# Keeping the low halves of the up weights in DRAM for the second half of the sequence

## The chip, the cores and the metric

The kernel runs on one core of a Trainium2 chip. The time is the device time of one execution in microseconds (us); smaller is better. The engines are TensorE (PE in the profile; PEld is its weight load), VectorE (DVE), ScalarE (ACT), GpSimd (POOL), and SyncE (SP), which here issues every DMA.

## The reference

One layer of a bidirectional hybrid encoder, in float32, for 2048 rows of width 1024:

```
mod = silu(c) @ w_ada + b_ada                       # shift1, scale1, gate1, shift2, scale2, gate2
u = adaln_modulate(x, shift1, scale1);  proj = u @ w_in
attn = rms_norm(gqa_attention(q, k, v))             # 8 query heads, 2 kv heads, axial rope
h = rms_norm(silu(layer_norm(depthwise_conv(a * sigmoid(g), width 31))) @ w_conv_pw2)
x = layer_norm(ALPHA * x + gate1 * (concat(attn, h) @ w_o))
u = adaln_modulate(x, shift2, scale2)
val, gt = split(depthwise_conv(u @ w_up, width 3))  # w_up: 1024 x 5632
x = layer_norm(ALPHA * x + gate2 * ((gelu(gt) * val) @ w_down))
```

The part that the change touches is `u @ w_up`, with the start of it inside the output projection `@ w_o` and the preparation of `w_down` beside it.

## The kernel before

Each float32 matrix product is made of three products of split numbers: an operand x is written as a high part (`wh` for weights, a rounded copy made by ACT, L124) and a low part (`wl`, x minus the high part, made by DVE, L127), and PE adds high*high, high*low and low*high.

The up projection and the down projection are block products of Strassen's kind: a 2 x 2 block product with seven products instead of eight (the numbers 0 to 6 are q in the code). A *set* is one block of this. In the up projection there are 44 sets: for each half of the sequence (1024 rows) 22 blocks of weights, each holding 128 gate columns and 128 value columns. The second half goes through the weight blocks in reverse order, so that sets 21 and 22 use the same block, whose prepared weights are kept in SBUF. A set has 7 products of 12 matmuls of 128 x 512.

- `wprep(n)` prepares the weights (the left operands) of set n. Two raw tiles `wr` of 512 KB come from `w_up`; DVE forms the sums and differences (`s`, and `wr` in place; L1068, L1071, L1072, L1082), and `put` splits each of the seven results into `wh` and `wl`. `run_set(n)` does the seven products and after each one calls the next step of `wprep(n + 1)`. The tiles `wh` and `wl` have seven buffers each, so the buffer of product q of the next set comes free when product q of this set is done.
- `evac` brings a finished product out of PSUM: DVE additions (L1126, L1129, L1133) and ACT copies (L1118, L1124).
- `post(n)` does the width-3 convolution, the GELU and the gate of the set before on ACT and DVE (L1139 to L1171) and stores the result `y` to `g_d`.
- `feed(q)` splits the right operand of product q (tiles `o`, from `stg`, four pieces of 128 x 512) for a whole half of the sequence. For the first half, operands 0 to 2 are made during the output projection (`ahead`), and operands 3 to 6 in set 0.
- `combine(1)` forms the right operands of the second half on POOL during sets 1 to 3 (`cb`, L917, L919). `down_ops` then scales the 22 row blocks of `w_down` on POOL, forms their sums and differences and stores them to `w_d` (L1187 to L1198); it goes one step after each product of even number, from set 3 on.

The output projection goes through 16 row tiles t. For each there are 48 matmuls (`out_mm`), then `norm1(t)` on DVE and ACT, and `second_in(t)`: eight transposes on PE, eight small ACT copies (`ut`) and a store to `u_d`. The last two `second_in` lie inside set 0.

The program is written with a framework that orders each engine's instructions by a simulated time; so each engine, and SP with its DMAs, has one fixed order, and an instruction that waits holds up those behind it on its engine. An operation placed earlier in the code can be placed much earlier on its engine, if its inputs allow.

Of the kernel before, what the change touches and what calls it, by code (L numbers as in the profile page):

```python
# [18 lines left out]
P = 128  # L19
# [7 lines left out]
NJ = DFF // P  # L27
# [6 lines left out]
def layer_kernel(ctx, tc, x, cT, w_ada, b_ada, b_adaT, w_in, qg2, kg2, rope, conv_t, cmask, mmask,  # L34
# [46 lines left out]
    def bank():  # L81
        return psp.tile([P, 512], F32, name="b", bufs=8)
# [112 lines left out]
    with ExitStack() as ph:  # L195
# [19 lines left out]
        wk = pool(ph, "wkA")  # L215
# [245 lines left out]
        bg = ada_later()  # L461
# [166 lines left out]
    def load_wo():  # L628
        wr = pool(wrx, "wr", "right")
        wp = pool(wox, "wpC", "right")  # L630
        for k in range(KD):
            woh.append(wp.tile([P, D], F32R, name="woh%d" % k))
            wol.append(wp.tile([P, D], F32R, name="wol%d" % k))
            for h in range(2):
                sl = slice(h * 512, (h + 1) * 512)
                raw = wp.tile([P, 512], F32, name="rw", bufs=4)
                SY.dma_start(raw, wo_d[h, k])
                yield
                split(woh[k][:, sl], wol[k][:, sl], raw)
# [309 lines left out]
    def load_left(n):  # L949
# [9 lines left out]
        for i, r in enumerate((rg, rv)):  # L959
            c0 = (t + 8 * i) * P  # L960
            for x in range(2):
                SY.dma_start(r[:, x * m:(x + 1) * m],
                             g_d[x * HJ + j0:x * HJ + j1, :, c0:c0 + P].rearrange("j p t -> p j t"))
                if t == 7 and i == 0:
                    V.tensor_copy(r[:, x * m:(x + 1) * m, P - 1], gf[:, x * HJ + j0:x * HJ + j1])

    cx = ExitStack()
    wk = pool(cx, "wkC")
    cs2 = ExitStack()
# [3 lines left out]
    def load_xt(t):  # L973
        xt = wk.tile([P, D], F32, name="xt", bufs=3)
        load_rows(xt, t)
        return xt
# [28 lines left out]
    def ahead():  # L1005
        load_left(0)
        for i in range(3):
            op_tiles(i, 4)
        yield from combine(0, stg, 5, True)

    bg = ahead()
    xs = {0: load_xt(0)}
    SY.dma_start(lg, ln1[0:1].broadcast_to([P, D]))
    SY.dma_start(lb, ln1[1:2].broadcast_to([P, D]))
# [4 lines left out]
    for t in range(NT):  # L1019
        if t == 5:  # L1020
            SY.dma_start(dww, dw_w)
            SY.dma_start(dwb, dw_b)
        if t >= 2:
            pss = out_mm(t)
        else:
            pss = pend[t]
        if 2 <= t < NT - 2:
            mixes["load"](t + 2)
        norm1(t, pss, xs[t])
        if t >= 10:  # L1030
            drain(bg, 6)
        if t >= 2:
            second_in(t - 2, xs.pop(t - 2))
            if t + 1 < NT:
                xs[t + 1] = load_xt(t + 1)
    drain(bg)
    wox.close()
    opools["b2"] = pool(b2x, "b2", "right")

# [12 lines left out]
    ws = pool(dx, "wsD", "right")  # L1052
    dl = ExitStack()
    NB = 960
    wops = {}

    def wprep(n):
        rg, rv = raws(n)
        m = 4 if n < NU else chunk_of(n)[1][1] - chunk_of(n)[1][0]
        s = ws.tile([P, 4, P], F32, name="s0", bufs=1)[:, 0:m]  # L1060
        a11, a12, a21, a22 = rg[:, 0:m], rg[:, m:2 * m], rv[:, 0:m], rv[:, m:2 * m]

        def put(i, src):
            w = [ws.tile([P, 4, P], F32R, name="w" + x, bufs=7)[:, 0:m] for x in "hl"]
            wops[n, i] = w
            split(*w, src)

        V.tensor_tensor(s, a21, a22, op=ALU.add)  # L1068
        put(0, a11)
        yield  # L1070
        (V if n < NU else G).tensor_tensor(a21, a11, a21, op=ALU.subtract)  # L1071
        V.tensor_tensor(a11, s, a11, op=ALU.subtract)  # L1072
        put(1, a11)
        yield
        put(3, a21)
        yield
        put(4, s)
        yield
        put(2, a12)
        yield  # L1080
        put(5, a22)
        (V if n < NU else G).tensor_tensor(a12, a12, a11, op=ALU.subtract)  # L1082
        yield
        put(6, a12)
        if n < 2:
            load_left(n + 1)
        if 0 < n < ND - 2 and n != NU:
            load_left(n + 2 if n + 2 != NJ else NJ + 2)
        yield

    def product(ps, a, b, nk, first):
        for k in range(nk):
            for x, y in ((0, 0), (0, 1), (1, 0)):
                T.matmul(ps, lhsT=a[x][:, k, :], rhs=b[y][k], start=first and k == 0 and (x, y) == (0, 0),  # L1094
                         stop=k == nk - 1 and x == 1, skip_group_check=True)

    def evac(q, z, c):


# [109 lines left out]
    def run_set(n, m, z, blocks, step):  # L1209

        wp = wprep(n + 1) if n + 1 < ND and n + 1 != NJ else iter(())
        z["b"] = [None] * 4
        for q in ORDER:
            x = "XYZW".index(bnk[q])
            first = z["b"][x] is None
            if first:
                z["b"][x] = bank()
            w = wops.pop((n, q))
            if n == NJ - 1:
                wops[NJ, q] = w  # L1220
            product(z["b"][x], w, ops[q], m, first)
            done = (q,) if n or q not in (4, 2, 5) else (4, 2, 5) if q == 5 else ()
            for i in done:
                evac(i, z, blocks(i))
                step(i)
            next(wp, None)

    drain(wprep(0))
    prev = iter(())
    feed = feeder(range(3, 7), 4, lambda i, k: half_src(0, i)[:, k], stg, "cb", 5, (3,))  # L1230
    for n in range(NU):
        h, j = set_of(n)
        hh = {}
        if n == 0:
            feed(3)

        def blocks(q):
            if q == 4:
                if n == 0:
                    second_in(NT - 1, xs[NT - 1])  # L1240
                    cs2.close()
                    cx.close()
                    opools["wkD"] = pool(dl, "wkD")
                    more_raws(opools["wkD"])
                for x in "gv":
                    hh[x] = opools["wkD"].tile([P, 1024 + 2 * HW], F32, name="h" + x, bufs=2 if x == "v" else 1)
                bg["h"] = hh["v"]
            return {(i, k): hh[x][:, HW + k * 512:HW + (k + 1) * 512] for i, x in enumerate("gv") if x in hh for k in (0, 1)}

        def step(q):  # L1250
            next(prev, None)
            if n in (NJ - 1, NU - 1):
                feed(q)
            if n == 0 and q in (0, 1, 3):
                feed({0: 4, 1: 5, 3: 6}[q])
            if "c" in bg and n != NJ - 1:
                if n < 3 or q % 2 == 0:
                    next(bg["c"], None)
            if n == 0 and q == 1:
                second_in(NT - 2, xs[NT - 2])  # L1260

        if n == NJ - 1:
            feed = feeder(ORDER, 4, lambda i, k: half_src(1, i)[:, k], opools["wkD"], "cb", 5, (1, 3))
        if n == NU - 1:
            feed = feeder(ORDER, chunks[0][1] - chunks[0][0], lambda i, k: w_d[i, :, chunks[0][0] + k], opools["wkD"], "cb", 5, ())
        run_set(n, 4, {}, blocks, step)
        if n == 0:
            bg["c"] = combine(1, opools["wkD"], 5)
        if n == 2:
            drain(bg["c"])  # L1270
            bg["c"] = down_ops()
        drain(prev)
        prev = post(n, hh["g"], hh["v"])
# [160 lines left out]
```

## Time and profile before

| | us |
|---|---|
| median of 3 runs | 2804.1 |
| lowest and highest run | 2801.17, 2805.29 |
| profiled execution, its own time | 2801.65 |
| its span, from first to last instruction | 2799.9 |
| PE busy in the span | 2670.3 (95%) |
| DVE busy in the span | 2187.2 (78%) |

The up projection runs from about 1426 to 2330 us, the down projection from there to the end. Busy shares are means over stages with different limits, so the stretches count: where PE has no gap, another engine that becomes faster gives nothing there.

### The profile page before, as it was taken

The numbers are of one execution on the slowest core, as the hardware profiler recorded it, in microseconds if no ns is written. First come the engines' busy times: TensorE is split into PE (matmuls) and PEld (weight loads), VectorE is DVE, ScalarE is ACT, GpSimd is POOL, SyncE is SP. The second block draws the span as 40 slices with busy tenths as digits, with TensorE's granted clock in tenths as the row PEclk, the third lists the DMA queues.
The fourth block names the chain that finished last, engine by engine and source line by source line (L and its number), as shares of the span: only waits on it lengthen the run. The fifth ranks groups of instructions, "written<-read, shape, count | busy, mean of one in ns | idle before, by whom it ended". The sixth has DMA issues, their size and how long they took to land. (4 is left out here: it accounts for less than half of the span.)

```text
span 2799.9 us, 35355 instructions
## 1 busy us (share of the span) xinstructions
PE 2670.3 (95%) x12108; PEld 2016.6 (72%) x12108; DVE 2187.2 (78%) x3161; ACT 1296.4 (46%) x2555; POOL 1277.5 (46%) x930
## 2 busy tenths in 40 slices
PE   6999999999999999999988999998999998999996
PEld 6787776766665665567866788887888886777774
DVE  6555466576858677837779999989898888989999
ACT  4333314445545455434454455455455555443542
POOL 3534338886867686833635212233231002336235
PEclk8999999999999999999999999999999999999998
DMA  8464232010101013026876433354444236545542
GB/s 265 124 203 146 85 78 54 22 34 19 27 16 35 23 37 105 14 53 179 237 223 217 137 127 128 127 184 137 136 143 150 76 102 218 154 127 154 171 142 69
DMA packets 339248, 327.41 MB, mean 117 GB/s; under 512 B 71150, under 2 KB 242542, under 8 KB 339068
## 3 DMA queue, kind: packets, MB, share of 16 engines
q1 hardware_dynamic: 339068, 325.15, 38.7%
q8 instruction: 95, 1.56, 0.2%
q14 instruction: 85, 0.70, 0.1%
HBM read 228.34 MB, written 96.74 MB: 116 GB/s over the span
## 5 line engine op out<-in xcount | busy, mean ns | idle before, releaser
L1094 PE MATMUL b<-o,wh 128*128 128x512 f32 x3696 | 1154.6, 397 | 45.6 <-ACT wh L124 13.2
L1094 PEld LDWEIGHTS b<-o,wh 128*128 128x128 f32 x3696 | 698.7, 190 | 214.5 <-ACT wh L124 21.8
L1094 PE MATMUL b<-o,wl 128*128 128x512 f32 x1848 | 718.4, 395 | 6.4 <-DVE wl L127 6.3
L124 ACT ACTIVATE wh<-wr 128x512 fp32r<-128x512 f32 (+2 forms) x450 | 248.2, 569 | 390.0 <-PE b L1094 213.3
L1094 PEld LDWEIGHTS b<-o,wl 128*128 128x128 f32 x1848 | 350.2, 190 | 90.4 <-DVE wl L127 11.9
L180 DVE TENSOR_REDUCE mm<-b 128x1 f32<-128x512 f32 x512 | 322.0, 682 | 117.8 <-PE b L178 116.0
L618 POOL TENSOR_TENSOR lp<-lp,pr 128x1024 f32<-128x1024 f32 x152 | 380.4, 2503 | 70.2 <-ACT pr L588 62.2
L588 ACT ACTIVATE pr<-b 128x512 f32<-128x512 f32 x512 | 278.6, 598 | 284.6 <-PE b L587 277.5
L127 DVE TENSOR_TENSOR wl<-wr,wh 128x512 fp32r<-128x512 f32 (+2 forms) x450 | 332.1, 749 | 14.6 <-ACT wh L124 13.6
L1190 POOL TENSOR_TENSOR cb<-cb,g 128x512 f32<-128x512 f32 x44 | 72.7, 1676 | 393.6 <-DMA cb<-in_w_down_dram 382.1
L597 PE MATMUL b<-pr,vt 128*64 128x512 f32 x1024 | 243.7, 606 | 1.8 <-ACT pr L588 1.8
L586 PE MATMUL b<-q,K 128*128 128x512 f32 x512 | 217.1, 426 | 7.0 <-DVE mm L180 3.4
L587 PE MATMUL b<-q,K 72*128 72x512 f32 x512 | 205.5, 403 | 3.1 <-DVE q L189 3.0
L178 PE MATMUL b<-K,q 128*128 128x512 f32 x512 | 164.6, 419 | 4.4 <-DVE mm L180 3.7
L597 PEld LDWEIGHTS b<-pr,vt 128*64 128x64 f32 x1024 | 66.4, 138 | 128.2 <-issue 111.2
L127 POOL TENSOR_TENSOR o<-stg,o 128x512 fp32r<-128x512 f32 x53 | 81.7, 1542 | 149.6 <-ACT o L124 149.1
L1071 POOL TENSOR_TENSOR wr<-wr,wr 128x384 f32<-128x384 f32 (+1 forms) x32 | 35.0, 1093 | 242.3 <-DVE s L1068 230.3
L124 ACT ACTIVATE o<-stg 128x512 fp32r<-128x512 f32 x177 | 107.6, 629 | 74.9 <-DMA stg<-w_d 53.9
L178 PEld LDWEIGHTS b<-K,q 128*128 128x128 f32 x512 | 92.2, 192 | 67.9 <-issue 34.1
L586 PEld LDWEIGHTS b<-q,K 128*128 128x128 f32 x512 | 98.9, 193 | 53.2 <-issue 19.5
L587 PEld LDWEIGHTS b<-q,K 72*128 72x128 f32 x512 | 99.2, 194 | 21.1 <-issue 3.4
L127 DVE TENSOR_TENSOR o<-stg,o 128x512 fp32r<-128x512 f32 x124 | 104.7, 861 | 5.5 <-ACT o L124 5.5
(260 smaller groups left out, 4899.8 us busy)
## 6 DMA issues: line engine op xcount, KB each, us to landing
wr<-in_w_up_dram SPq DMA_DIRECT2D x86, 512.0 KB, 4.2
stg<-w_d SPq DMA_DIRECT2D x133, 256.0 KB, 3.3
g_d<-y SPq DMA_DIRECT2D x44, 512.0 KB, 2.6
w_d<-cb SPq DMA_DIRECT2D x77, 256.0 KB, 2.3
wr<-g_d SPq DMA_DIRECT2D x96, 192.0 KB, 2.5
ar<-in_w_ada_dram SPq DMA_DIRECT2D x64, 256.0 KB, 3.0
cb<-in_w_down_dram SPq DMA_DIRECT2D x44, 256.0 KB, 2.7
x<-in_x_dram SPq DMA_DIRECT2D x32, 256.0 KB, 3.9
```

Source lines behind the costliest of these rows:

```text
L124: A.activation(hi, src, AF.Copy)
L127: (el or V).tensor_tensor(lo, src, hi.bitcast(F32), op=ALU.subtract)
L178: T.matmul(px, lhsT=q1[:, i * P:(i + 1) * P], rhs=K1[:, g, kc * 512:(kc + 1) * 512], start=True, stop=True)
L180: V.tensor_reduce(mm[:, h * 4 + i, kc:kc + 1], px, axis=AX, op=ALU.max)
L586: T.matmul(ps, lhsT=k1, rhs=m1, start=True, stop=False)
L587: state["s"] = T.matmul(ps, lhsT=k2, rhs=m2[0:72], start=False, stop=True).ins
L588: ex = state["exp"] = A.activation(pr[:, i, :], ps, AF.Exp, scale=0.125).ins
L597: state["pv"] = T.matmul(po[i * 64:(i + 1) * 64, :], lhsT=vt[:, kt, g * 64:(g + 1) * 64], rhs=pr[:, i, :], start=kt == 0, stop=kt == NT - ...
L618: eng.tensor_tensor(acc, acc, pr, op=ALU.add)
L1071: (V if n < NU else G).tensor_tensor(a21, a11, a21, op=ALU.subtract)
L1094: T.matmul(ps, lhsT=a[x][:, k, :], rhs=b[y][k], start=first and k == 0 and (x, y) == (0, 0), stop=k == nk - 1 and x == 1, skip_group_check ...
L1190: G.tensor_tensor(b[i, k], b[i, k], g2[:, k * 512:(k + 1) * 512], op=ALU.mult)
```

## The change

Three edits.

1. A DRAM buffer `wl_d` is added. While sets 0 to 20 of the first half are prepared, each of the seven low parts is also stored to it (147 stores of 256 KB). For sets 23 to 43 `put` loads the low part from it (147 loads of 256 KB) in place of the DVE subtraction. High parts, sums and differences are made as before.
2. `wprep(0)` moves from after the output projection to beside its row tiles 12 and 13 (two of its seven steps), with four tiles of the pool `wp` for the weights of products 0 and 1. These two products are placed right behind the last row tile. Set 0 then does products 2 to 6 in the order 2, 3, 4, 5, 6 (it was 0, 1, 3, 4, 2, 5, 6), and `second_in(14)` moves from after product 1 to after product 3.
3. `down_ops` starts after set 6 (it was after set 2).

```diff
+    wl_d = dram.tile([NJ, 7, P, 512], F32, name="wl_d")
...
         def put(i, src):
-            w = [ws.tile([P, 4, P], F32R, name="w" + x, bufs=7)[:, 0:m] for x in "hl"]
+            if n == 0 and i < 2:
+                w = [mixes["wp"].tile([P, 4, P], F32R, name="w0", tag="rw", bufs=4) for _ in "hl"]
+            else:
+                w = [ws.tile([P, 4, P], F32R, name="w" + x, bufs=7)[:, 0:m] for x in "hl"]
             wops[n, i] = w
-            split(*w, src)
+            if n >= NU:
+                split(*w, src)
+                return
+            low = w[1].bitcast(F32)
+            j = set_of(n)[1]
+            at = wl_d[j, i].rearrange("p (k c) -> p k c", c=P)
+            if n < NJ:
+                split(*w, src)
+                if n < NJ - 1:
+                    SY.dma_start(at, low)
+            else:
+                SY.dma_start(low, at)
+                A.activation(w[0], src, AF.Copy)
...
     bg = ahead()
+    w0 = wprep(0)
...
+        if t in (12, 13):
+            next(w0)
...
     drain(bg)
+    z0 = [None] * 4
+    for q in range(2):
+        z0[q] = bank()
+        product(z0[q], wops.pop((0, q)), ops[q], 4, True)
     wox.close()
...
-        z["b"] = [None] * 4
-        for q in ORDER:
+        z["b"] = [None] * 4 if n else z0
+        for q in ORDER if n else range(7):
...
-            w = wops.pop((n, q))
+            w = wops.pop((n, q)) if n or q > 1 else None
...
-            product(z["b"][x], w, ops[q], m, first)
-            done = (q,) if n or q not in (4, 2, 5) else (4, 2, 5) if q == 5 else ()
+            if w is not None:
+                product(z["b"][x], w, ops[q], m, first)
+            done = (q,) if n or q not in (2, 4) else (4, 2) if q == 4 else ()
...
-    drain(wprep(0))
+    drain(w0)
...
-            if n == 0 and q == 1:
+            if n == 0 and q == 3:
                 second_in(NT - 2, xs[NT - 2])
...
         if n == 2:
             drain(bg["c"])
+            bg.pop("c")
+        if n == 6:
             bg["c"] = down_ops()
```

How the order of the instructions changes is shown at three places. First ACT, at the end of the output projection and the start of set 0 (`xt` and `ut` belong to `second_in`, `wh<-wr` and `wh<-s` to `wprep(0)`, `o` to the right operands). Before:

```order
L989 ACTIVATE xt<-z,l_n,l_r 128x1024
L124 ACTIVATE wh<-wr_10436 128x512
L124 ACTIVATE o_12644<-stg 128x512 x3
L124 ACTIVATE o_12646<-stg 128x512
L998 ACTIVATE ut<-b,md 128x128 x8
L124 ACTIVATE o_12679<-stg 128x512
L1124 ACTIVATE p_12677<-b 128x512
L124 ACTIVATE o_12679<-stg 128x512
```

and after:

```order
L1048 ACTIVATE xt<-z,l_n,l_r 128x1024
L1057 ACTIVATE ut<-b,md 128x128 x8
L125 ACTIVATE wh<-wr_10438 128x512
L125 ACTIVATE wh<-s_12235 128x512
L125 ACTIVATE wh<-wr_10437 128x512
L125 ACTIVATE wh<-wr_10438 128x512
L125 ACTIVATE o_12678<-stg 128x512 x3
L125 ACTIVATE o_12680<-stg 128x512
```

The first pieces of right operand 3 (the first `o` rows) now stand behind the eight copies of `second_in(13)` and four high parts. PE has between its last output transposes and these pieces the 24 matmuls of products 0 and 1.

Second SP, from the last store of the output projection on (`wl_d<-wl` are the new stores, `wr` the raw weights of set 1, `stg` the right operands). Before:

```order
L985 DMA x_d<-z 128x1024
L889 DMA stg<-t_d 128x512 x2
L1001 DMA u_d<-ut 512x1x128
L955 DMA wr_10437<-in_w_up_dram 128x8x128
L889 DMA stg<-u_d 128x512
```

and after:

```order
L1044 DMA x_d<-z 128x1024
L992 DMA wl_d<-wl 128x512 x4
L957 DMA wr_10438<-in_w_up_dram 128x8x128
L891 DMA stg<-t_d 128x512 x5
L1060 DMA u_d<-ut 512x1x128
```

Four stores, each of which waits for a subtraction of DVE, now stand ahead of the refills of `stg` (eleven in all), and so does the first raw tile of set 1; before, seven of the refills stood ahead of that tile.

Third DVE, in set 22, the first of the second half (`wl` are the low parts, `o` the right operands of the second half, `u` and `hv` the evacuation). Before:

```order
L127 TENSOR_TENSOR wl<-wr_10436,wh 128x512
L127 TENSOR_TENSOR o_16407<-stg,o_16406 128x512
L1152 SCALAR_TENSOR_TENSOR y<-hv,dww,y 128x1023
L127 TENSOR_TENSOR o_16438<-stg,o_16437 128x512
L1133 TENSOR_TENSOR hv<-b,u_16518 128x512
L127 TENSOR_TENSOR wl<-wr_10437,wh 128x512
L127 TENSOR_TENSOR o_16438<-stg,o_16437 128x512
L127 TENSOR_TENSOR wl<-s_16475,wh 128x512
L1171 TENSOR_TENSOR y<-y 128x1024
L127 TENSOR_TENSOR wl<-wr_10436,wh 128x512
```

and after:

```order
L128 TENSOR_TENSOR o_16527<-stg,o_16526 128x512
L1176 SCALAR_TENSOR_TENSOR y<-hv,dww,y 128x1023
L128 TENSOR_TENSOR o_16558<-stg,o_16557 128x512
L1157 TENSOR_TENSOR hv<-b,u_16640 128x512
L128 TENSOR_TENSOR o_16558<-stg,o_16557 128x512
L997 TENSOR_TENSOR s_16755<-wr_12864 128x512
L1195 TENSOR_TENSOR y<-y 128x1024
```

The low parts are gone from DVE; the rest keeps its order but for `s`.

## Rows read from the trace of the kernel before

**Rows 1.** The page, part 1: busy time, share of the span, instructions.

```profile
PE 2670.3 (95%) x12108; PEld 2016.6 (72%) x12108; DVE 2187.2 (78%) x3161; ACT 1296.4 (46%) x2555; POOL 1277.5 (46%) x930
```

**Rows 2.** Stretches: length, busy (x instructions), granted clock, DMA share, GB/s.

```profile
1426.00:1450.00 24.00, 18.32 (x68) 13.86 (x68) 20.71 (x35) 17.51 (x37) 7.53 (x8) 0.86 0.73 217
1450.00:1470.00 20.00, 18.20 (x82) 14.42 (x82) 11.56 (x19) 11.93 (x26) 1.29 (x1) 1.00 0.62 177
...
1485.00:1505.00 20.00, 15.09 (x52) 11.51 (x51) 18.84 (x20) 10.14 (x18) 11.04 (x7) 0.83 0.66 217
1505.00:1550.00 45.00, 39.83 (x169) 31.11 (x168) 44.61 (x45) 20.45 (x46) 23.81 (x13) 1.00 0.62 194
...
1600.00:1800.00 200.00, 200.00 (x871) 163.37 (x871) 186.40 (x222) 101.90 (x210) 46.08 (x27) 1.00 0.39 130
...
1890.00:1906.00 16.00, 12.33 (x45) 9.26 (x45) 14.31 (x14) 12.67 (x28) 8.61 (x6) 0.89 0.41 126
1906.00:1920.00 14.00, 14.00 (x62) 11.42 (x61) 13.97 (x14) 4.05 (x8) 9.71 (x7) 1.00 0.63 206
1920.00:1945.00 25.00, 20.30 (x82) 16.11 (x81) 24.83 (x31) 13.58 (x28) 2.11 (x1) 0.93 0.34 112
1945.00:2300.00 355.00, 355.00 (x1545) 289.97 (x1545) 307.28 (x386) 180.25 (x374) 56.11 (x33) 1.00 0.37 118
...
2330.00:2350.00 20.00, 15.83 (x59) 12.15 (x60) 14.02 (x27) 7.77 (x18) 2.48 (x3) 0.91 0.72 230
```

**Rows 3.** Timeline, PE: start, length; in brackets idle before it and its releaser.

```profile
1429.48 0.73 PE L1094 MATMUL b<-o,wh 128*128 128x512 f32 x2 [3.67 <-ACT wh L124]
...
1492.01 0.87 PE L1094 MATMUL b<-o,wh 128*128 128x512 f32 x2 [2.58 <-ACT p L1124]
...
1925.64 0.98 PE L1094 MATMUL b<-o,wh 128*128 128x512 f32 x2 [4.70 <-DVE u L1129]
...
2332.16 1.19 PE L1094 MATMUL b<-o,wh 128*128 128x512 f32 x2 [2.98 <-DVE ac L1109]
```

**Rows 4.** Timeline, ACT and DVE, start of set 0.

```profile
1428.81 0.61 ACT L124 ACTIVATE wh<-wr 128x512 fp32r<-128x512 f32 x1
...
1431.41 2.88 ACT L998 ACTIVATE ut<-b,md 128x128 f32<-128x128 f32 x8
...
1437.24 1.17 ACT L124 ACTIVATE wh<-wr 128x512 fp32r<-128x512 f32 x2
...
1441.49 1.27 DVE L127 TENSOR_TENSOR wl<-wr,wh 128x512 fp32r<-128x512 f32 x2
```

**Rows 5.** Timeline, DVE and POOL: idle DVE, and DVE beside POOL.

```profile
1251.67 1.29 DVE L982 SCALAR_TENSOR_TENSOR z<-xt,b 128x512 f32<-128x512 f32 x2 [7.98 <-DMA xt<-in_x_dram]
...
1471.52 0.69 DVE L127 TENSOR_TENSOR wl<-wr,wh 128x512 fp32r<-128x512 f32 x1 [5.87 <-ACT wh L124]
...
1536.85 8.45 POOL L1197 TENSOR_TENSOR cb<-cb 128x512 f32<-128x512 f32 x4
...
1542.36 1.79 DVE L127 TENSOR_TENSOR wl<-wr,wh 128x512 fp32r<-128x512 f32 x1
...
1550.44 0.68 DVE L127 TENSOR_TENSOR wl<-s,wh 128x512 fp32r<-128x512 f32 x1
```

**Rows 6.** Groups of DVE instructions, 1945 to 2300: busy, mean ns, idle before.

```profile
L127 DVE TENSOR_TENSOR wl<-wr,wh 128x512 fp32r<-128x512 f32 x110 | 83.2, 764 | 1.3 <-ACT wh L124 0.8
```

**Rows 7.** Waits of SP's queue, 1945 to 2300: total, times, longest.

```profile
SPq L1172 <- DVE y L1171: 142.4, 17, 13.5
```

**Rows 8.** DMA, 1426 to 1550: 40 slices, share, landing times.

```profile
GB/s 251 0 157 211 367 206 258 331 244 5 85 75 268 304 322 358 194 163 270 169 85 78 325 250 302 330 187 220 134 264 305 150 0 170 276 156 321 265 170 61
...
q1 hardware_dynamic: 24847, 25.61, 66.4%
...
wr<-in_w_up_dram SPq DMA_DIRECT2D x12, 512.0 KB, 4.5
...
stg<-t_d SPq DMA_DIRECT2D x7, 256.0 KB, 3.2
```

More of the change, by code (lines that the diff above doesn't have):

```diff
@@ L650, in load_wo @@
         mixes["load"] = load_mix
+        mixes["wp"] = wp
         mixes["raw"] = [wr.tile([P, KD, P], F32, name="wr%d" % i) for i in range(2)]
@@ L965, in load_left, with wprep, put, product @@
                     V.tensor_copy(r[:, x * m:(x + 1) * m, P - 1], gf[:, x * HJ + j0:x * HJ + j1])
+    wops = {}
+    def wprep(n):
+        rg, rv = raws(n)
+        m = 4 if n < NU else chunk_of(n)[1][1] - chunk_of(n)[1][0]
+        s = (ws if n else wk).tile([P, 4, P], F32, name="s0", bufs=1)[:, 0:m]
+        a11, a12, a21, a22 = rg[:, 0:m], rg[:, m:2 * m], rv[:, 0:m], rv[:, m:2 * m]
+        def put(i, src):
+            if n == 0 and i < 2:
+                w = [mixes["wp"].tile([P, 4, P], F32R, name="w0", tag="rw", bufs=4) for _ in "hl"]
+            else:
+                w = [ws.tile([P, 4, P], F32R, name="w" + x, bufs=7)[:, 0:m] for x in "hl"]
+            wops[n, i] = w
+            if n >= NU:
[11 more added lines that the diff above has]
+                A.activation(w[0], src, AF.Copy)
+        V.tensor_tensor(s, a21, a22, op=ALU.add)
+        put(0, a11)
+        yield
+        (V if n < NU else G).tensor_tensor(a21, a11, a21, op=ALU.subtract)
+        V.tensor_tensor(a11, s, a11, op=ALU.subtract)
+        put(1, a11)
+        yield
+        put(3, a21)
+        yield
+        put(4, s)
+        yield
+        put(2, a12)
+        yield
+        put(5, a22)
+        (V if n < NU else G).tensor_tensor(a12, a12, a11, op=ALU.subtract)
+        yield
+        put(6, a12)
+        if n < 2:
+            load_left(n + 1)
+        if 0 < n < ND - 2 and n != NU:
+            load_left(n + 2 if n + 2 != NJ else NJ + 2)
+        yield
+    def product(ps, a, b, nk, first):
+        for k in range(nk):
+            for x, y in ((0, 0), (0, 1), (1, 0)):
+                T.matmul(ps, lhsT=a[x][:, k, :], rhs=b[y][k], start=first and k == 0 and (x, y) == (0, 0),
+                         stop=k == nk - 1 and x == 1, skip_group_check=True)
     cx = ExitStack()
@@ L1054, in layer_kernel @@
     NB = 960
[L1055 to L1063, printed above, removed]
-            w = [ws.tile([P, 4, P], F32R, name="w" + x, bufs=7)[:, 0:m] for x in "hl"]
-            wops[n, i] = w
-            split(*w, src)
[L1068 to L1095, printed above, removed]
     def evac(q, z, c):
```

## The prediction

> **What bounds the kernel now.** I read the page's busy times first: PE is busy for 2670 of 2800 us [rows 1], so only PE's gaps can be won, and an engine that gets work off its hands helps only where PE waits for it. The stretches of the up projection come next [rows 2]. From 1600 to 1800 and from 1945 to 2300 PE has no gap; its pitch there is 200/871 = 0.230 us a matmul, a set of 84 takes 19.3 us. So most of the 147 subtractions that leave DVE are taken from a stretch in which PE never waits: from 1945 to 2300 alone they are the larger part of the 83 us of the biggest DVE group [rows 6], and there they give nothing.
>
> The loss lies at the seams. With PE's instructions of each stretch at 0.230 us (the 16 transposes too, a little too much for them), PE should have needed 15.6 of 24 us from 1426, 18.8 of 20 from 1450, 11.9 of 20 from 1485, 38.8 of 45 from 1505, 10.3 of 16 from 1890, 18.8 of 25 from 1920 and 13.5 of 20 from 2330 [rows 2]. Lost are 8.4 + 1.2 = 9.6 us at the start of set 0, 8.1 + 6.2 = 14.3 us in sets 1 to 4, 5.7 us in set 21, 6.2 us between sets 22 and 23, and 6.5 us at the end of the up projection: 42 us in all. The timeline names the waits [rows 3]: the first high part of set 0 (3.67 us), an ACT evacuation (2.58), the DVE evacuation `u` (4.70), a DVE addition (2.98). Each gap costs more than itself: the stretch from 1426 with two gaps has a mean clock of 0.86, which is 6.7 us at the lower level of 1.2 GHz [rows 2], so 3.4 us at half pace, or 1.7 us lost, for each gap.
>
> **The change part by part.** *Products 0 and 1 ahead.* PE's last transposes end at 1425.8, 3.67 us before the first product [rows 3]. With the weights ready, 24 matmuls go on without a gap, to 1425.8 + 5.5 = 1431.3. Next PE needs right operand 3. ACT is free at 1428.8 [rows 4], then has eight `ut` copies (2.75 us), four high parts (0.53 us each) and the first `o` copy: 1434.2. DVE, at 0.6 us a subtraction [rows 4], has four low parts from about 1432.2, one difference, then the first `o`: about 1436.2. Between 1431.3 and 1436.2 PE has only eight transposes and a matmul (1.3 us), so it idles 3.6 us; with 1.7 us for the clock and 1 us for the refills of `stg`, which now stand behind the new stores, 6.3 us are lost in place of 9.6. Gain 3 us. The bounds: 9.6 us if nothing is late, and minus 3 us if the refills (3.2 us to land [rows 8]) chain up for the four operands.
>
> The four DVE instructions that move into the output projection (0.6 us each, 2.4 us) fall where DVE stood idle for 7.98 us [rows 5]: nothing; without that cover they would cost their 2.4 us once.
>
> *Sets 1 to 4.* Here DVE is the limit: 18.84 of 20 and 44.61 of 45 us busy [rows 2]. It gets three things: the 2.4 us above; part of an idle time of 5.87 us, in which it waited for a high part whose raw tile was late [rows 5] and which is now asked for ahead of eleven refills; and from edit 3 the absence of POOL's eight down-weight operations up to 1545. Beside such an operation (8.45/4 = 2.1 us) a low part took 1.79 us, alone 0.68 [rows 5]: 1.1 us each, 8.8 us for eight. The sum is up to 17 us of relief against 14.3 us lost, but PE comes 3 us earlier, the sixteen operations of `combine` remain, and the 8.8 us come after the worst stalls. I take 5 us; bounds 0 and 14.3.
>
> The Trainium skill, "SBUF — State Buffer", section "SBUF: two separate sides", says that a DVE instruction with two SBUF inputs and a GpSimd one that reads SBUF share a lock, and the second to start waits out the whole of the first. By that rule a pair could cost DVE the full 2.1 us, 17 us for eight in place of 8.8, and edit 3 alone could clear this place. The trace shows 1.1 us more on the low part, and I go by that.
>
> *Set 22.* Before, DVE is busy 13.97 of 14 and 24.83 of 25 us here [rows 2], and PE waits 4.70 us for an evacuation queued behind the seven low parts of set 23 [rows 3]. These leave DVE: 7 x 0.68 = 4.8 us by the lone duration, 7 x 1.79 = 12.5 us at most; the mean of 0.764 us in the second half [rows 6] makes 5.3. By the deferral POOL also has fewer down-weight operations here (it is busy 9.71 of 14 us from 1906 [rows 2]). So the gap and its slow clock go: 6.2 us. Of the 5.7 us in set 21, one low part lies in the way; I count 1 us, bounds 0 and 5.7. Together 7 us, bounds 3 and 11.9.
>
> *End of the up projection.* At most two low parts of set 43 lie in the busy stretch ahead of the gap: 1 us, bounds 0 and 3.
>
> *What is added.* 147 stores and 147 loads of 256 KB, all on SP's queue. A store waits for its subtraction and holds up what stands behind it (raw tiles, `y`); the raw tiles are asked for two sets ahead, so the steady sets cover this. A load waits for PE to finish the same product one set earlier, and is needed six products later, 72 x 0.230 = 16.5 us; less 3.2 us to land [rows 8], 13.3 us of slack cover it. Only in sets 0 to 4 do the stores meet a busy DMA: 66% of the engines' time [rows 8]. Forty stores (10.5 MB) less the eleven down-weight transfers that move away (2.9 MB) are 7.6 MB, 21 us at the 367 GB/s of the fastest slice, against 0.34 x 124 = 42 us free. I charge 2 us; bounds 0 and the third rival's price.
>
> Sum: -3 - 5 - 7 - 1 + 2 = -14 us, against the profiled execution's own 2801.65 us: 2787.7. The median of the runs is 2.45 us above that execution; on that scale it is 2804.1 - 14 = 2790.
>
> **The rivals.** *DVE gives the start back* (0.20). PE's early products are lost again, since in sets 1 to 4 DVE sets the pace and its worst stalls come before edit 3 has effect; only set 22 and the end remain: -7 - 1 + 2 = -6, 2798 us. For it: DVE is 99% busy from 1505; against it: 5.87 us of DVE idle at 1471.
>
> *All DVE stalls go* (0.10). The lock between DVE and POOL costs more than I charge, and place two and set 21 clear entirely: -3 - 14.3 - 11.9 - 1 = -30, 2774 us. Against it: `combine` is still there.
>
> *The stores starve set 2* (0.12), the slower side. From 1426 to 1471, when set 2's raw tiles land, nineteen stores (5.0 MB, 13.6 us at 367 GB/s) must fit beside shares of 0.73 and 0.62 [rows 2], that is into about 14 us of free time. If they do not, the raw tiles come up to 13.6 us later, PE stalls as long, with 1.7 us of slow clock, and the 8 us of the first two places are not won: -14 + 8 + 15.3 = +9, 2813 us. It decides once the share stays near 1.0 from 1440 to 1475. For it: slices of 0 GB/s beside slices of 367 [rows 8] show a queue that blocks; against it: the raw tile of set 1 is now asked for earlier, and `combine` can yield.
>
> *The low parts come late in the second half* (0.10). SP waits up to 13.5 us, 8.4 us in the mean, for `y` once in a set [rows 7], and loads that stand behind that store have 13.3 us of slack. With half a microsecond of stall in each of 21 sets the gain shrinks by 10.5: 2800 us. Against it: DVE has more time there, so `y` comes earlier.
>
> *The seams stay as they are* (0.05): the two early products meet the same wait one product later and set 22 finds another releaser; 2804 us.
>
> **How the numbers follow.** The forecast, 2790 us, has 0.43, with a range of its own of 2783 to 2796 from the bounds of its terms. About 0.2%, or 5.6 us, is what a measurement of this kernel can tell from no change: below 2798.5 us is faster. Faster: 0.43 + 0.10 + half of the first rival and a third of the fourth, 0.66. Slower, above 2809.7: most of the third, 0.11. The same: 0.23. The range from 2779 to 2808 leaves out most of the second and of the third rival.
>
> **What would show it.** In the new profile PE should have no gap between the last transposes of the output projection and 5 us into set 0, then one of 3 to 5 us that waits for a right operand; in sets 2 to 4 fewer waits for `u` and `p`; no wait for `u` at the start of set 23; DVE busy well under 80% from set 24 on, with PE still without a gap. It is wrong if PE waits for a DMA of `wl` in the second half, if raw tiles are waited for in sets 1 to 3, or if the gap in set 22 stays with DVE idle.

## The result and the profile after

The changed kernel takes 2789.34 us (median of 6 runs, 2784.77 to 2795.68), the kernel before 2803.8 us (6 runs, 2801.17 to 2805.29): a ratio of 0.9948 (95% 0.9936 to 0.9959), 14.5 us faster. Forecast were 14 us and 2790 us. A second set of runs (e1 below) has 2784.47 against 2802.03 us, 17.6 us faster (0.9935). The profiled execution of the changed kernel was the slowest of the six (2795.68 us, span 2793.9 us), so 6 us of what it shows is not the change; the second trace has a span of 2782.5 us.

In the new trace the helper lines have moved: the product is L1023 (before L1094), the evacuations `u` L1150 and L1153 (L1126, L1129), the subtraction of DVE L128 (L127). Page, part 1, of the changed kernel; DVE has lost 147 instructions and 101 us of [rows 1], PE next to nothing:

```profile
PE 2673.7 (96%) x12108; PEld 2019.2 (72%) x12108; DVE 2086.4 (75%) x3014; ACT 1295.7 (46%) x2555; POOL 1268.5 (45%) x930
```

The stretches that answer to [rows 2] (length, busy and instructions of PE, PEld, DVE, ACT, POOL, granted clock, DMA share, GB/s), changed kernel:

```profile
1426.00:1450.00 24.00, 18.32 (x77) 14.52 (x76) 20.83 (x34) 18.74 (x40) 8.28 (x9) 0.86 0.73 228
1450.00:1470.00 20.00, 19.95 (x91) 15.89 (x90) 15.14 (x23) 13.68 (x31) 4.64 (x3) 1.00 0.90 286
1470.00:1485.00 15.00, 15.00 (x67) 12.25 (x66) 11.07 (x14) 6.49 (x14) 5.02 (x4) 1.00 1.08 361
1485.00:1505.00 20.00, 18.64 (x82) 14.93 (x81) 19.90 (x20) 9.25 (x19) 9.25 (x5) 1.00 0.80 265
1505.00:1550.00 45.00, 39.52 (x165) 31.50 (x164) 44.83 (x50) 22.69 (x46) 12.68 (x8) 0.96 0.78 263
1880.00:1900.00 20.00, 16.28 (x70) 12.76 (x69) 14.24 (x17) 14.07 (x31) 10.07 (x8) 1.00 0.71 240
1900.00:1940.00 40.00, 40.00 (x169) 32.53 (x168) 34.19 (x35) 22.47 (x50) 15.06 (x10) 0.96 0.74 243
1940.00:2290.00 350.00, 350.00 (x1523) 285.77 (x1523) 228.72 (x254) 178.45 (x368) 64.67 (x41) 1.00 0.72 224
2320.00:2345.00 25.00, 18.98 (x74) 14.35 (x73) 17.98 (x33) 8.86 (x20) 4.51 (x4) 0.93 0.64 203
```

PE is still idle for 5.5 us from 1505, where DVE is as full as before. It has no gap from 1900 to 1940, where DVE is no longer full. From 1940 to 2290 DVE fell from 87 to 65%, but PE had no gap there before either. PE's timeline, changed kernel (start, length; in brackets idle before and its releaser), against [rows 3]:

```profile
1431.57 5.84 PE L1023 MATMUL b<-o,w 128*128 128x512 f32 x24
1440.35 0.50 PE L1023 MATMUL b<-o,wh 128*128 128x512 f32 x1 [2.94 <-ACT o L125]
...
1444.45 0.79 PE L1023 MATMUL b<-o,wh 128*128 128x512 f32 x1 [2.74 <-DVE o L128]
...
1521.55 1.22 PE L1023 MATMUL b<-o,wh 128*128 128x512 f32 x2 [4.91 <-DVE u L1153]
...
1898.62 0.70 PE L1023 MATMUL b<-o,wh 128*128 128x512 f32 x2 [2.70 <-DVE u L1153]
```

The 24 early matmuls go on without a gap; then right operand 3 is late twice, as forecast. In sets 2 to 4 PE has three gaps where it had five, but one for `u` is longer (4.91).

The gap of 2.70 us is not what is left of the 4.70 us of [rows 3]. Counted by PE's product matmuls (84 a set, from set 0), set 22 of the kernel before runs from 1879.3 to 1903.5 and set 23 to 1930.3, so the wait of 4.70 us before 1925.64 lies in set 23, as PE sees it; the prediction speaks of set 22, in which the program prepares set 23's weights. Set 23 of the changed kernel has no gap. The 2.70 us lie in set 22, which had two gaps before:

```profile
1895.01 0.71 PE L1094 MATMUL b<-o,wh 128*128 128x512 f32 x2 [1.77 <-DVE u L1129]
...
1900.64 0.50 PE L1094 MATMUL b<-o,wh 128*128 128x512 f32 x1 [1.90 <-DVE o L127]
```

The transfers that edit 1 added (from issue to landing, median us; two more stores stand under the name of the tiles of products 0 and 1 of set 0), and the waits of SP's queue from 1940 to 2290 (total, times, longest), changed kernel:

```profile
wl<-wl_d SPq DMA_DIRECT2D x147, 256.0 KB, 3.1
wl_d<-wl SPq DMA_DIRECT2D x145, 256.0 KB, 3.9
```

```profile
SPq L994 <- PE b L1023: 180.2, 96, 4.2
...
SPq L1196 <- DVE y L1195: 2.1, 5, 1.5
```

SP now waits for PE to free a low part's tile (96 times, 4.2 us at most), no longer 13.5 us for `y` [rows 7], and PE waits for none of the loads.

To see where time is won, I read from each trace when PE starts the first matmul of a set (84 product matmuls each). At PE's pitch of 0.230 us a set takes 19.3 us, five 96.6, three 58. Times in us; "start" is from PE's last transposes of the output projection to set 1:

| kernel | start | sets 1-5 | sets 21-23 | of these 21, 22, 23 | set 24 | ratio (95%) |
|---|---|---|---|---|---|---|
| before | 33.1 | 111.5 | 70.4 | 19.4, 24.2, 26.8 | 19.3 | 1 |
| changed, e1 again | 29.8, 30.1 | 105.8, 105.5 | 66.1, 64.9 | 21.7, 25.1, 19.3; 22.8, 22.8, 19.3 | 19.3, 19.4 | 0.9948 (0.9936-0.9959), e1 0.9935 (0.9921-0.9949) |
| e2 edit 1 alone | 34.7 | 107.0 | 66.6 | 19.7, 26.1, 20.8 | 19.3 | 0.9984 (0.9973-0.9994) |
| e3 edit 2 alone | 30.0 | 115.1 | 72.4 | 19.3, 24.5, 28.6 | 19.3 | 1.0005 (0.9995-1.0016) |
| e4 edit 3 alone | 34.5 | 107.3 | 63.8 | 19.4, 24.3, 20.1 | 21.0 | 0.9975 (0.9967-0.9984) |
| e5 edits 1, 3 | 36.6 | 101.3 | 67.0 | 20.2, 27.4, 19.3 | 19.3 | 0.9963 (0.9951-0.9975) |
| e6 edits 2, 3 | 30.1 | 109.1 | 67.4 | 23.3, 23.9, 20.2 | 21.0 | 0.9974 (0.9962-0.9986) |
| e7 edit 3 from set 8 | 33.7 | 108.9 | 71.1 | 19.7, 23.5, 27.9 | 19.3 | 0.9985 (0.9975-0.9995) |
| e8 combine written later | 29.7 | 105.7 | 65.2 | 21.7, 24.2, 19.3 | 19.3 | 0.9943 (0.9930-0.9955) |
| e9 combine held, quiet | 30.0 | 96.7 | 64.9 | 20.3, 24.3, 20.3 | 19.3 | 0.9918 (0.9905-0.9932) |
| e10 e9 without edit 1 | 28.2 | 96.5 | 63.7 | 19.5, 24.1, 20.1 | 19.3 | 0.9925 (0.9913-0.9938) |
| e11 low parts of set 23 only | 28.2 | 109.8 | 65.2 | 23.1, 22.8, 19.3 | 19.7 | 0.9962 (0.9948-0.9976) |
| e12 e9 without edit 2 | 36.3 | 96.8 | 66.2 | 21.5, 25.4, 19.3 | 19.3 | 0.9956 (0.9943-0.9968) |

Sets 6 to 20 take 289.5 us in every trace. e2, e5 and e12 do the same operations up to set 1 and have starts of 34.7, 36.6 and 36.3 us: 2 us between two single traces can be chance.

### The profile page after: what moved, and what is told of

Its sections match the earlier page's. It is cut to its first block, busy times and chain, and to the rows that moved or that the text cites. A ratio compares the mean times of both kernels' runs of the same rounds, so it can differ in the third digit from the quotient of the medians.

```text
span 2793.9 us, 35859 instructions
## 1 busy us (share of the span) xinstructions
PE 2673.7 (96%) x12108; PEld 2019.2 (72%) x12108; DVE 2086.4 (75%) x3014; ACT 1295.7 (46%) x2555; POOL 1268.5 (45%) x930
## 5 line engine op out<-in xcount | busy, mean ns | idle before, releaser
L1023 PE MATMUL b<-o,wh 128*128 128x512 f32 x3680 | 1149.4, 396 | 40.4 <-DVE u L1153 10.7
L1023 PEld LDWEIGHTS b<-o,wh 128*128 128x128 f32 x3680 | 694.6, 189 | 207.1 <-ACT wh L125 11.7
L1023 PE MATMUL b<-o,wl 128*128 128x512 f32 x1840 | 716.7, 395 | 5.4 <-DVE wl L128 5.3
L1023 PEld LDWEIGHTS b<-o,wl 128*128 128x128 f32 x1840 | 348.5, 189 | 88.4 <-DVE wl L128 10.4
L125 ACT ACTIVATE wh<-wr 128x384 fp32r<-128x384 f32 (+2 forms) x322 | 169.3, 546 | 275.9 <-PE b L1023 125.3
L1214 POOL TENSOR_TENSOR cb<-cb,g 128x512 f32<-128x512 f32 x44 | 62.3, 1442 | 457.1 <-DMA cb<-in_w_down_dram 455.9
L128 DVE TENSOR_TENSOR wl<-wr,wh 128x384 fp32r<-128x384 f32 (+2 forms) x322 | 228.6, 722 | 7.8 <-ACT wh L125 7.3
L179 PEld LDWEIGHTS b<-K,q 128*128 128x128 f32 x512 | 92.2, 192 | 70.4 <-issue 34.9
L128 POOL TENSOR_TENSOR o<-stg,o 128x512 fp32r<-128x512 f32 x53 | 80.8, 1526 | 136.7 <-ACT o L125 129.7
L995 ACT ACTIVATE wh<-wr 128x512 fp32r<-128x512 f32 x126 | 77.3, 625 | 96.2 <-PE b L1023 92.2
L588 PEld LDWEIGHTS b<-q,K 72*128 72x128 f32 x512 | 98.9, 193 | 20.8 <-issue 3.4
L128 DVE TENSOR_TENSOR o<-stg,o 128x512 fp32r<-128x512 f32 x124 | 106.7, 879 | 9.4 <-ACT o L125 9.4
## 6 DMA issues: line engine op xcount, KB each, us to landing
wr<-g_d SPq DMA_DIRECT2D x96, 192.0 KB, 2.8
```

Of the source, the lines that this page charges most:

```text
L179: T.matmul(px, lhsT=q1[:, i * P:(i + 1) * P], rhs=K1[:, g, kc * 512:(kc + 1) * 512], start=True, stop=True)
L588: state["s"] = T.matmul(ps, lhsT=k2, rhs=m2[0:72], start=False, stop=True).ins
L995: A.activation(w[0], src, AF.Copy)
L1214: G.tensor_tensor(b[i, k], b[i, k], g2[:, k * 512:(k + 1) * 512], op=ALU.mult)
```

## The experiments

### e1: the changed kernel again

> The changed kernel once more, as a control. In its first trace PE's last transposes of the output projection end 6.0 us later than before, 4.7 us of it lost at the end of the attention (a gap of 2.12 us and a slow stretch) and in the output projection 3.1 us between the wait for osq and the last transposes (194.7 against 191.6 us). If this is chance, a second trace has the 191.6 us again and a span some 6 us shorter, near 2788 us. Rival: the two preparation steps of edit 2 slow the output projection, and the 194.7 us come again. Median either way 2788 to 2791 us.

No edit. 2784.47 us, ratio 0.9935, below the 2788 to 2791 us expected. From the last `osq` product (the end of the attention) to the last transposes the output projection took 187.8 us (first trace 193.7, before 190.8): chance, and edit 2 does not slow it. The kernels without edit 2 have 190.8 to 193.2, those with it 187.2 to 193.7. Whether edit 2 shortens it is open: five of the eight traces with edit 2 lie below all six without. The two windows show what the chance is (columns as above), first trace and second trace of the changed kernel:

```profile
1225.00:1260.00 35.00, 33.58 (x139) 24.51 (x138) 12.99 (x15) 6.49 (x11) 8.73 (x6) 0.90 0.30 76
```

```profile
1225.00:1260.00 35.00, 33.58 (x153) 24.82 (x153) 15.94 (x18) 5.39 (x8) 10.29 (x5) 1.00 0.45 111
```

Both have the same gap of 1.42 us and the same 33.58 us of busy PE, but the first gets 14 matmuls fewer done: its granted clock is 0.90 in the mean, so for a part of the stretch it was at the lower level of 1.2 GHz, and in the second trace never.

### e2, e3, e4: each edit alone

From the changed kernel, edit 1 is taken out like this:

```diff
...
-            if n < NJ:
-                split(*w, src)
-                if n < NJ - 1:
-                    SY.dma_start(at, low)
-            else:
-                SY.dma_start(low, at)
-                A.activation(w[0], src, AF.Copy)
+            split(*w, src)
```

edit 2 like this (with `wprep(0)` back behind the output projection):

```diff
-        if t in (12, 13):
-            next(w0)
...
-        product(z0[q], wops.pop((0, q)), ops[q], 4, True)
...
-        for q in ORDER if n else range(7):
+        for q in ORDER:
```

and edit 3 like this:

```diff
         if n == 2:
             drain(bg["c"])
-            bg.pop("c")
-        if n == 6:
             bg["c"] = down_ops()
```

e2 is without 2 and 3, e3 without 1 and 3, e4 without 1 and 2.

> Edit 1 alone. My theory: the seven low parts of set 23 on DVE are the cause of the gap in set 22, so set 22 takes about 19.3 us (26.8 before) and all later sets stand 7 us earlier; the stores cost sets 0 to 4 up to 3 us; 2798 us. Rival: POOL's down-weight operations, not the low parts, are the cause; then the gap stays and the time is 2804 to 2807 us.

> Edit 2 alone. My theory: products 0 and 1 ahead gain 3 us up to the start of the second set, and this holds at the start of set 5 and to the end: 2801 us. Rival: DVE sets the pace in sets 1 to 4 and takes it back: 0 us at the start of set 5, 2804 us. Second rival: the early products are worth more without the stores ahead of the refills: 5 us, 2799 us.

> Edit 3 alone. My theory: sets 2 to 4 lose 15 us before; without POOL's down-weight operations there they lose about 9, and set 22 keeps its gap of 5 us and its 26.8 us: 2798 us. Rival: POOL beside DVE is also the cause at set 22, and both go: 2791 us. Second rival: the gain of sets 1 to 4 comes from edit 2 and not from here: 2804 us.

Where these texts, and those of e6 and e7, put the gap in set 22, it is set 23 of the table.

Edit 1 alone: 2799.26 us; the gap is gone as the theory says (set 23 falls from 26.8 to 20.8 us, and 1.9 come back in set 22). POOL's eight down-weight operations still stand there, and PE waits for 0.85 of the 20 us (columns as above), e2:

```profile
1901.00:1921.00 20.00, 19.15 (x82) 14.91 (x81) 18.66 (x17) 9.01 (x22) 17.39 (x9) 1.00 0.84 274
```

The start loses 1.6 us, but sets 1 to 5, where the theory expected a loss too, gain 4.5.

Edit 2 alone: 2803.68 us, no change: the rival. In the trace 3.1 us are won at the start and 3.7 lost again in sets 1 to 5, and sets 21 to 23 lose 2.0 more. Sets 1 to 5, before and then e3:

```profile
1458.94:1570.42 111.48, 101.39 (x421) 80.59 (x420) 102.41 (x114) 53.02 (x113) 42.70 (x24) 0.97 0.60 190
```

```profile
1454.57:1569.71 115.14, 104.80 (x421) 83.70 (x420) 107.97 (x116) 53.69 (x112) 43.72 (x25) 0.93 0.59 184
```

PE's idle time there is the same (10.1 and 10.3 us); DVE is busy for 5.6 us more, and PE is slower, with a granted clock of 0.93 in place of 0.97. So that DVE's pace takes the 3 us back fits, but this trace does not separate it from the clock; that nothing is left is shown by the twelve runs.

Edit 3 alone: 2795.12 us; sets 1 to 5 gain 4.1, and, against the theory, the gap of set 23 is gone (20.1 us) although DVE still has set 23's seven low parts (1.7 us come back in set 24). POOL's timeline there shows why, e4:

```profile
1899.16 1.94 POOL L127 TENSOR_TENSOR o<-stg,o 128x512 fp32r<-128x512 f32 x1 [1.56 <-ACT o L124]
1915.56 1.90 POOL L1191 TENSOR_TENSOR cb<-cb,g 128x512 f32<-128x512 f32 x1 [14.46 <-DMA cb<-in_w_down_dram]
1924.65 5.68 POOL L1191 TENSOR_TENSOR cb<-cb,g 128x512 f32<-128x512 f32 x3 [7.19 <-ACT p L1125]
```

POOL leaves DVE alone for 14.46 and 7.19 us there, where it did eight operations before.

### e5, e6: two edits of three

e5 is the changed kernel with edit 2 out, e6 with edit 1 out. Of e5's diff the core, then of e6's:

```diff
-        product(z0[q], wops.pop((0, q)), ops[q], 4, True)
```

```diff
-                    SY.dma_start(at, low)
...
-                SY.dma_start(low, at)
```

> Edits 1 and 3 without 2. In the traces so far edit 2 alone gains 3 us up to the second set and loses 3.7 us in the next five, since DVE sets the pace there. My theory: with POOL's down-weight operations gone DVE has room, so the 3 to 4 us of edit 2 stay in the changed kernel and are missing here: start of set 0 34 us (30 with edit 2), the five sets after it 106 us; 4 us slower than the changed kernel, a ratio of 0.9955. Rival: they are given back also there, the five sets take 103 us and the ratio is that of the changed kernel, 0.994.

> Edits 2 and 3 without 1. Edit 3 alone took the gap of 4.7 us out of set 22. Rival to my prediction: the loads of edit 1 then have nothing left to win there; sets 21 to 23 take 64 to 66 us as with all three and the ratio is 0.994 to 0.995. My theory as predicted: the low parts of set 23 still cost 3 to 5 us in DVE's queue; sets 21 to 23 take 69 us, ratio 0.996.

e5: 2793.55 us, 4 to 8 us slower than the changed kernel by the ratios. Edit 2 is missed (theory), but only in part: the start takes 6.5 to 6.8 us more than with it, and sets 1 to 5 give 4.2 to 4.5 back (101.3 us, the side of the rival, which expected 103). In these traces 2.3 us of edit 2 are left. e6: 2794.99 us, 7 to 11 us slower. Sets 21 to 24 take 88.4 us where the two traces of the changed kernel have 85.4 and 84.3, the theory's side (2.6 us of it in sets 23 and 24); and sets 1 to 5 take 3.3 to 3.6 us more, which neither had expected.

### e7: the same operations in another place

```diff
-        if n == 6:
+        if n == 8:
             bg["c"] = down_ops()
```

on e4.

> Edit 3 alone, but the down-weight operations begin after set 8 in place of 6. Three sets make one round of their twelve steps, so from 8 on they stand against set 22 as in the kernel before (after 2), while sets 1 to 5 stay free of them as with 6. Theory of place: set 22 had its gap because eight POOL operations fell on DVE's busiest 20 us; then the gap is back, sets 21 to 23 take 70 us (63.8 with 6) and the ratio is 0.9985. Rival: the operations were merely too many, not in the wrong place; then it runs like edit 3 alone, 0.9975. Sets 1 to 5: 107 us by both.

2798.67 us, ratio 0.9985, sets 21 to 23 71.1 us: the theory of place. POOL and PE of e7:

```profile
1900.64 1.28 POOL L1191 TENSOR_TENSOR cb<-cb,g 128x512 f32<-128x512 f32 x1 [0.41 <-DMA cb<-in_w_down_dram]
1904.38 4.99 POOL L1191 TENSOR_TENSOR cb<-cb,g 128x512 f32<-128x512 f32 x3 [2.46 <-DMA cb<-in_w_down_dram]
1909.31 3.44 POOL L1198 TENSOR_TENSOR cb<-cb 128x512 f32<-128x512 f32 x2
1915.66 3.54 POOL L1198 TENSOR_TENSOR cb<-cb 128x512 f32<-128x512 f32 x2 [2.90 <-DMA w_d<-cb]
```

```profile
1922.73 1.22 PE L1007 MATMUL b<-o,wh 128*128 128x512 f32 x2 [5.21 <-DVE u L1130]
```

Eight POOL operations on DVE's fullest 20 us, and the wait for `u` is back at 5.21 us (4.70 in [rows 3]).

### e8, e9: combine later

```diff
-                if n < 3 or q % 2 == 0:
+                if q % 2 == 0 or n > 24:
...
-        if n == 0:
+        if n == 4:
             bg["c"] = combine(1, opools["wkD"], 5)
-        if n == 2:
+        if n == 9:
             drain(bg["c"])
             bg.pop("c")
-        if n == 6:
+        if n == 9:
             bg["c"] = down_ops()
```

and for e9 also

```diff
                     b[i, j] = pl.tile([P, 512], F32, name="cb", bufs=n)
+                    if h and i + j == 0:
+                        A.activation(b[i, j][:, 0:1], bg["h"][:, HW + 512:HW + 513], AF.Copy)
...
-            if "c" in bg and n != NJ - 1:
+            if "c" in bg and n not in (NJ - 1, NJ, NJ + 1):
```

> The changed kernel with combine put behind set 4 (sets 5 to 9, four steps a set) and the down weights behind set 9, at seven steps a set from set 25 on. Theory: what is left of the stalls in sets 1 to 5 (9 us) is POOL's sixteen combine operations beside DVE, each 1.1 us longer for DVE; the five sets take 98 to 100 us (105.6) and the time falls by 6 to 8 us against the changed kernel, ratio 0.991. Rival: DVE has a backlog from the start of set 0 and simply too much to do there; the five sets keep 104 us or more, and the ratio stays 0.994. Second rival: the stalls move to sets 5 to 9, which now have no gap.

> The last experiment wrote combine behind set 4, but its POOL operations stood at 1476 to 1535 us as before, so it tried nothing. Here each of combine's four rounds also waits for a result of set 4 and later, and no down weight is prepared in sets 22 and 23 (seven steps a set from set 25 on). Theory: what is left of the stalls is POOL's two-input operations beside DVE; sets 1 to 5 take 98 to 101 us (105.6) and sets 21 to 24 82 to 84 us (84.3 to 85.4); 6 to 8 us faster than the changed kernel, ratio 0.991. Rival: a backlog of DVE from the start of set 0; sets 1 to 5 keep 104 us or more, ratio 0.994.

e8 tried nothing in sets 1 to 5: the scheduler put combine where its data allowed. POOL's first operation of combine in e8, then in e9:

```profile
1476.72 3.27 POOL L919 TENSOR_TENSOR cb<-cb 128x512 f32<-128x512 f32 x2 [11.53 <-DMA cb<-u_d]
```

```profile
1529.33 1.65 POOL L921 TENSOR_TENSOR cb<-cb 128x512 f32<-128x512 f32 x1 [72.35 <-DMA cb<-u_d]
```

e9, with combine really held (and, as in e10 and e12, no down weights in sets 21 to 23): 2780.4 us, 0.9918, with e10 below the fastest kernel of this study. Sets 1 to 5 of the changed kernel, then of e9, then two pieces of the latter:

```profile
1461.60:1567.37 105.77, 98.93 (x421) 79.52 (x420) 100.58 (x117) 53.45 (x112) 29.00 (x17) 0.98 0.80 269
```

```profile
1451.82:1548.54 96.72, 96.72 (x422) 78.79 (x421) 88.99 (x116) 53.51 (x113) 8.08 (x5) 1.00 0.69 226
```

```profile
1480.00:1500.00 20.00, 20.00 (x89) 16.32 (x88) 19.89 (x28) 12.85 (x27) 0.00 (x0) 1.00 0.64 218
1500.00:1520.00 20.00, 20.00 (x88) 16.32 (x87) 19.30 (x26) 11.73 (x26) 0.00 (x0) 1.00 0.67 215
```

PE has no gap in sets 1 to 5; all 9 us of stall there are gone. DVE is 99% busy in the first piece as it was in the changed kernel (19.90 of 20 from 1485), but it does 28 instructions in that time and not 20. Over sets 1 to 5 as a whole the count is nearly the same, 116 and 117, and DVE's busy time is 11.6 us less with twelve POOL operations fewer: its busy time was partly waiting for POOL, by estimate about 1 us for each of them. So the rival of a backlog is out. Holding combine also moves its transfers out of these sets (DMA share 0.69 and 0.80); no run separates the two, and that it is POOL rests on the longer durations of DVE beside POOL ([rows 5], and the rows at the end of the next section). The sets 21 to 23 did not gain further (64.9; 84.2 with set 24, where 82 to 84 were expected); what holds them is not settled, POOL's subtractions for the right operands being still there.

### e10: is edit 1 needed?

```diff
-                    SY.dma_start(at, low)
...
-                SY.dma_start(low, at)
```

on e9, as in e6.

> The same without edit 1: no low part goes through DRAM. Theory: stores and subtractions are only two ways to the same end, and with POOL away from both busy places the low parts of edit 1 win nothing: sets 1 to 5 as with edit 1 (98 to 101 us), sets 21 to 24 within 1.5 us of it, ratio 0.991 to 0.992. Rival, as predicted: the seven low parts of set 23 are in the way of the evacuation by themselves; sets 21 to 24 are 3 to 5 us longer than with edit 1, ratio 0.9925.

2780.59 us: level with e9. Sets 1 to 5 and 21 to 24 (82.9 against 84.2) lose nothing without edit 1. The theory holds, with one reserve: the ratio, 0.9925, is the rival's number, though not for the rival's reason. The later sets, where the down weights now run at seven steps a set, take 3.2 us more than in e9 (396.9 against 393.7 from set 25 to the 84th matmul of the down projection). That edit 1 would buy room there is argued from one trace of each.

### e11: seven low parts in place of 147

```diff
-            if n < NJ:
+            if n < NJ or not (j == NJ - 2):
                 split(*w, src)
-                if n < NJ - 1:
+                if n < NJ - 1 and (j == NJ - 2):
```

> The changed kernel with only seven of the 147 low parts through DRAM, those that set 23 loads. Prediction: the other 140 take work off DVE where PE never waits, so sets 21 to 23 keep their 65 to 66 us and nothing is lost there or later; ratio 0.994 as the changed kernel. Theory from e2 and e6: the stores also hold up combine on SP's queue and so spread its POOL operations over sets 1 to 4; without them sets 1 to 5 take 109 us as without edit 1 (105.6 with it), ratio 0.9955.

2792.24 us, ratio 0.9962. Sets 21 to 23 keep their 65.2 us: the prediction. Sets 1 to 5 take 109.8: the theory from e2 and e6. The first and the last operations of combine, changed kernel, then e11:

```profile
1479.74 3.33 POOL L919 TENSOR_TENSOR cb<-cb 128x512 f32<-128x512 f32 x2 [12.36 <-DMA cb<-u_d]
...
1533.43 3.85 POOL L921 TENSOR_TENSOR cb<-cb 128x512 f32<-128x512 f32 x2
```

```profile
1472.36 3.01 POOL L919 TENSOR_TENSOR cb<-cb 128x512 f32<-128x512 f32 x2 [10.54 <-issue]
...
1512.97 3.31 POOL L921 TENSOR_TENSOR cb<-cb 128x512 f32<-128x512 f32 x2
```

With the stores on SP's queue combine's sixteen operations spread over 57.5 us and not 43.9. So it is in every trace: 57.5 to 61.2 us with the stores of sets 0 to 20 (the changed kernel, e1, e2, e5, e8), 42.5 to 43.9 without, as long as combine is not held. Four comparisons agree that sets 1 to 5 are then shorter, by 3.3 to 6.0 us (e2 against before, the changed kernel against e6 and e11, e5 against e4). Against e6 and e11, 1.0 to 2.7 us of that is idle time of PE; the rest is the granted clock (0.98 and 0.97 against 0.95). That the spreading is what helps, and not something else that the stores do, is argued; only the gain is shown.

### e12: edit 2 where DVE has room

```diff
-        product(z0[q], wops.pop((0, q)), ops[q], 4, True)
```

on e9, as in e5.

> e9 without edit 2. In e9 PE has no gap in sets 1 to 5, which take 96.7 us. Theory: a gain ahead of a stretch lasts only if the stretch's engine has room; with POOL away it has, so the early products' 4 to 6 us at the start of set 0 (30.0 us from the last transposes to set 1 with them, 33 to 37 without) are all missing here and sets 1 to 5 stay at 97 us: ratio 0.9935 to 0.9945 (e9 0.9918). Rival: they are taken back also here (sets 1 to 5 shorter, or a later gap smaller), ratio 0.992.

2789.31 us, ratio 0.9956, against e9's 0.9918. The start takes 36.3 us, sets 1 to 5 still 96.8. Nothing is given back: the theory. That the difference is larger than expected has a part that the edit need not explain: 4.8 us lie in the output projection (192.0 against 187.2), which varies by that much (e1).

## Why the prediction was right

The sum was right: -14 us forecast, -12.3 and -14.5 in the two traces, from the last transposes to the end of the first set of the down projection. In part this is luck. Sets 1 to 5 gained 2.7 to 3.0 us more than their terms (-5, and +2 for the stores), and the sets from 21 on 2.5 to 4.8 us less than theirs (-8); the two errors cancel. The mechanisms that were named are there, but the reasons of two terms do not hold.

*Products 0 and 1 ahead*: -3 forecast, -3.3 and -3.0 measured at the start, by the mechanism given. The two gaps are 5.7 us, where 3.6 and 1 for the refills were charged. But what lasts of it depends on the other edits: alone it is worth nothing (e3); in the full change, where e5 loses 6.5 to 6.8 us at the start and has 4.2 to 4.5 back in sets 1 to 5, some 2.3 us; with DVE relieved 6 us (e12). So the rival in which DVE gives the start back is what happens to edit 2 by itself, and for the larger part it happens in the full change too. The total stays below that rival's 2798 us because sets 1 to 5 gain for other reasons.

*Sets 1 to 4*: -5 forecast, with the stores -3; -5.7 and -6.0 measured, sets 1 to 5. Edit 3 alone makes -4.1 of it (e4), as forecast, since POOL's operations lengthen DVE's. Failed is the step "I charge 2 us" for the added stores: with edits 2 and 3 in place they win 3.3 to 4.3 us there (e6, e11). A cost shows only at the start, and without edit 2: 1.6 and 2.1 us (e2 against before, e5 against e4), no more than chance can make. No term had a gain from the stores. The moved 2.4 us and the earlier raw tiles were not tested apart; from 1450 to 1550 ACT's waits for raw tiles fell from 7.9 us to 3.5 and 1.9, and PE waited for none.

*Set 22*: -7 forecast with set 21, -4.3 and -5.4 measured, sets 21 to 23. By PE's count the gap lies in set 23, and the 5.7 us put down to set 21 lie in set 22. Set 23 fell from 26.8 to 19.3 us, 7.5 us where 6.2 were forecast. The step "So the gap and its slow clock go" because the seven low parts leave DVE is half the cause. Two loads met there: seven low parts and eight POOL operations that lengthen what DVE does. Either one away removes the gap (e2, e4), both together gain 1.5 to 2.5 us more in sets 23 and 24, and the POOL operations put back in that place bring it back (e7). What fails in size is the 1 us for "set 21": set 22 takes 25.1 and 22.8 us (24.2 before), and set 21 itself, which had lost nothing, takes 21.7 and 22.8 (19.4 before). No term had that loss. It stands in e6 and e11 too (23.3 and 23.1), and in none of the edits alone (19.3 to 19.7); why it comes is open.

*End of the up projection*: -1 forecast; from set 25 to the end of the first set of the down projection it takes 392.9 and 391.8 us, 391.9 before: nothing.

*Rivals.* The stores did not starve set 2: the DMA share was 0.90 and 1.08 from 1450 to 1485, and PE had no gap from 1470 to 1485. The low parts did not come late: 350 of 350 us busy. That most of the 147 subtractions win nothing was right (e11).

What ties the parts together is POOL beside DVE. All 88 evacuations `hv<-b,u`, which read `b` from PSUM, stay at 0.68 us, those beside a POOL operation too, while `y<-y`, with both inputs in SBUF, reaches 2.31 (changed kernel; durations in ns, least, median, most, then first and last start):

```profile
L1157 DVE TENSOR_TENSOR hv<-b,u x88: 672/682/692, 1468.5 to 2311.2; 128x512 f32<-128x512 f32 x88
```

```profile
L1195 DVE TENSOR_TENSOR y<-y x44: 1207/1214/2310, 1495.7 to 2325.0; 128x1024 f32<-128x1024 f32 x44
```

The Trainium skill, "SBUF — State Buffer", section "SBUF: two separate sides", names DVE instructions with two inputs from SBUF among those that share a lock with GpSimd. These two rows agree. The extra is 1.1 us here at most, as in [rows 5], less than a whole POOL operation of 1.3 to 2 us, the most that this rule would give; yet e9, with twelve POOL operations fewer in sets 1 to 5 (17 and 5), has 9 us of stalls less there.

## What to carry to other kernels

A gain is worth what the next busy engine leaves of it: test each edit alone and without it, since one that shows nothing alone (edit 2) can be worth 6 us once that engine has room (e12). Name the set of a gap by the engine that waits: the prediction took DVE's set for PE's. Read the instructions done per stretch, not only the busy share: 99% of DVE was 20 instructions in 20 us beside POOL and 28 without. Where a seam stalls, first ask which background work stands there; holding it back by a real dependency won as much without the 294 transfers of edit 1 (e10) as with them (e9).

## What the runs showed of the hardware

The same gap of PE is followed by a slow stretch in one execution and not in the next (0.90 in the first trace of the changed kernel and 1.00 in the second, after 1.42 us of idle in both); that made 14 matmuls or 3.2 us. No edit touches the attention, yet its last `osq` product began between 1231.2 and 1238.1 us in the fourteen traces. The changed kernel's six runs scatter over 11 us, in e1 over 8, so one trace of it is not its median.
